# Fewer, larger tail loads in a pooling kernel, with one square moved to VectorE

## Chip, cores, metric

One core of a Trainium2 chip. Times are device microseconds of a whole execution; the profile's span is some 1.7 to 1.8 us shorter. Every run was fast, with a granted clock of 1.0.

## The reference

```python
x: (32, 256, 4096) float32, p = 2.0, kernel_size = 4
for i in range(out_length):
    window = np.abs(x[:, :, 4 * i:4 * i + 4]) ** p
    result[:, :, i] = (np.mean(window, axis=-1)) ** (1.0 / p)
```

Each output is the root of the mean of four squares. It reads 134.22 MB and writes 33.55 MB.

## The kernel before

The input is cut into 20 slots of at most 13184 columns on 128 partitions, which rotate through three SBUF tiles. ScalarE (ACT) squares in place, VectorE (DVE) sums fours, ACT takes the root of a whole group (`groups` says how many loads make one), and the result is stored. An odd piece (840 columns' worth, laid out as 3584 columns on 30 partitions) goes first.

```python
slots = [[(W, [W])]] * 17 + [[(W, [6592, 6592])]]            # W = 13184
slots += [[(6592, [6592]), (6592, [6592])], [(6592, [6592]), (4216, [2112, 2104])]]
ODD = 840
groups = [2] * 9 + [3, 1]
late = {7, 8, 9, 10}            # groups whose store waits on the load queue, after all loads
in_x = {9: (2, 0), 10: (2, 4944)}
FINE, ENDS, LAG = {21}, {19, 20}, 1
PAIRS = 15                      # from this load on: two pairwise adds instead of a reduce
# ...
for i in range(n):
    s, _, w, chunks = loads[i]
    while ahead < n and loads[ahead][0] < s + X_SLOTS:
        load(ahead)             # one DMA on the sync queue
        ahead += 1
    # ...
    for step in chunks:
        v = xs[i][:, c:c + step]
        r = nc.scalar.activation(out=v, in_=v, func=Act.Square)
        # ...
        total_sum(ots[g][:, summed:summed + step // k], v, i)
        while pending and pending[0][0] <= done - LAG:
            root(*pending.pop(0)[1:])
        # ...
for job in pending:
    root(*job[1:])
for g in sorted(late):
    store(g, nc.sync)
```

The tail, which the change touches, is the last two slots (numbers 18 and 19) and the four late stores.

Of the kernel before, what the change touches and what calls it, by code (L numbers as in the profile page):

```python
# [1 line left out]

# [4 lines left out]


@with_exitstack
def kernel(  # L10
    ctx: ExitStack,
    tc: tile.TileContext,
    x: bass.AP,
    p: float,
    kernel_size: int,
    out: bass.AP,
):








    nc = tc.nc

    assert float(p) == 2.0, "kernel specialized for p == 2"
    k = int(kernel_size)
    assert k == 4, "kernel specialized for kernel_size == 4"  # L30

    P = nc.NUM_PARTITIONS
    fp32 = mybir.dt.float32
    Act = mybir.ActivationFunctionType
    xf = x.rearrange("b c l -> (b c l)")
    of = out.rearrange("b c l -> (b c l)")
    total = xf.shape[0] // P

    W, O_W = 13184, 6592
    X_SLOTS, O_SLOTS = 3, 2  # L40
    slots = [[(W, [W])]] * 17 + [[(W, [6592, 6592])]]
    slots += [[(6592, [6592]), (6592, [6592])], [(6592, [6592]), (4216, [2112, 2104])]]
    ODD = 840
    groups = [2] * 9 + [3, 1]
    late = {7, 8, 9, 10}
    in_x = {9: (2, 0), 10: (2, 4944)}
    FINE, ENDS, LAG = {21}, {19, 20}, 1
    PAIRS = 15


    loads = [(s, sum(w for w, _ in slot[:j]), *slot[j]) for s, slot in enumerate(slots)
             for j in range(len(slot))]
    n = len(loads)
    assert sum(w for _, _, w, _ in loads) + ODD == total

    firsts = [sum(groups[:g]) for g in range(len(groups))]
    assert sum(groups) == n
    group_of = [g for g, count in enumerate(groups) for _ in range(count)]
    columns = [sum(w for _, _, w, _ in loads[firsts[g]:firsts[g] + groups[g]])
               for g in range(len(groups))]  # L60

    x_pool = ctx.enter_context(tc.tile_pool(name="x_pool", bufs=1))
    o_pool = ctx.enter_context(tc.tile_pool(name="o_pool", bufs=1))

    x_tiles = [x_pool.tile([P, W], fp32, name=f"xt{j}") for j in range(X_SLOTS)]
    o_tiles = [o_pool.tile([P, O_W], fp32, name=f"ot{j}") for j in range(O_SLOTS)]
    ctx.enter_context(tc.manual_schedule())

    def block(flat, g, div):
        at, width = sum(columns[:g]) * P // div, columns[g] * P // div  # L70
        return flat[at:at + width].rearrange("(p w) -> p w", p=P)

    xs = {}
    by_load = []

    def load(i):
        s, at, w, _ = loads[i]
        v = x_tiles[s % X_SLOTS][:, at:at + w]
        g = group_of[i]
        src = sum(loads[j][2] for j in range(firsts[g], i))  # L80
        nc.sync.dma_start(out=v, in_=block(xf, g, 1)[:, src:src + w])  # L81
        xs[i] = v

    ots = {}




    stores = {}
    by_act = []  # L90
    sums = []

    def follows(ins, before):
        for b in before:
            tc.declare_no_dep(ins.ins, b.ins, reason="follows from other waits")

    def store(g, queue):
        stores[g] = queue.dma_start(out=block(of, g, k), in_=ots[g])  # L98

    def root(g, o, ends):  # L100
        r = nc.scalar.activation(out=o, in_=o, func=Act.Sqrt, scale=1.0 / k)  # L101
        follows(r, by_act[:-1] + list(stores.values()))
        by_act.append(r)
        if ends and g not in late:
            store(g, nc.scalar)

    def total_sum(o, v, i):
        add = mybir.AluOpType.add
        if i < PAIRS:
            r = nc.vector.tensor_reduce(  # L110
                out=o, in_=v.rearrange("p (n j) -> p n j", j=k),
                axis=mybir.AxisListType.X, op=add,
            )
            follows(r, sums[:-1])
            sums.append(r)
            return

        q = v.rearrange("p (n j) -> p n j", j=k)
        front = v[:, 0:v.shape[1] // 2]
        h = front.rearrange("p (n j) -> p n j", j=2)  # L120
        r = nc.vector.tensor_tensor(out=h, in0=q[:, :, 0:2], in1=q[:, :, 2:4], op=add)  # L121
        follows(r, sums[:-1] + by_load)
        r = nc.vector.tensor_tensor(out=o, in0=h[:, :, 0], in1=h[:, :, 1], op=add)  # L123
        follows(r, sums[:-1])
        sums.append(r)


    Q = 30
    odd = ODD * P // Q
    t = o_tiles[1][0:Q, 0:odd]  # L130
    nc.sync.dma_start(out=t, in_=xf[(total - ODD) * P:total * P].rearrange("(p w) -> p w", p=Q))  # L131
    ahead = 0
    while ahead < n and loads[ahead][0] < X_SLOTS:
        load(ahead)
        ahead += 1
    nc.vector.tensor_tensor(out=t, in0=t, in1=t, op=mybir.AluOpType.mult)  # L136
    o = o_tiles[1][0:Q, odd:odd + odd // k]
    nc.vector.tensor_reduce(  # L138
        out=o, in_=t.rearrange("p (n j) -> p n j", j=k),
        axis=mybir.AxisListType.X, op=mybir.AluOpType.add,  # L140
    )
    nc.scalar.activation(out=o, in_=o, func=Act.Sqrt, scale=1.0 / k)  # L142
    stores["odd"] = nc.scalar.dma_start(
        out=of[(total - ODD) * P // k:total * P // k].rearrange("(p w) -> p w", p=Q), in_=o,
    )
    pending = []
    done = 0
# [3 lines that stand above are left out]
            load(ahead)  # L151
            ahead += 1
        g = group_of[i]
        if i == firsts[g]:
            t, first = (o_tiles[g % O_SLOTS], 0) if g not in in_x else (x_tiles[in_x[g][0]], in_x[g][1])
            ots[g] = t[:, first:first + columns[g] // k]
            summed = rooted = 0
        assert sum(chunks) == w
        c = 0
        for step in chunks:  # L160
            v = xs[i][:, c:c + step]
            r = nc.scalar.activation(out=v, in_=v, func=Act.Square)  # L162
            follows(r, by_act[:-1])
            by_act.append(r)
            total_sum(ots[g][:, summed:summed + step // k], v, i)
            while pending and pending[0][0] <= done - LAG:
                root(*pending.pop(0)[1:])
            done += 1
            c += step
            summed += step // k  # L170
            ends = summed == columns[g] // k
            if ends or i in FINE or (i in ENDS and c == w):
                pending.append((done - 1, g, ots[g][:, rooted:summed], ends))
                rooted = summed
# [6 lines that stand above are left out]
# [1 line left out]
_INS = ['x', 'p', 'kernel_size']  # L182
_OUTS = [((32, 256, 1024), 'float32')]

_NUMBERS = {'p': 2.0, 'kernel_size': 4}


# [26 lines left out]
```

## Time and profile before

| | before |
|---|---|
| time, median of the first 3 runs | 395.49 us (394.0 to 395.52) |
| profiled run, its span | 394.21 us, 392.4 us |
| DVE / ACT busy | 268.5 us (68%) / 280.2 us (71%) |
| bytes moved, mean rate | 167.77 MB, 428 GB/s |
| DMAs | 35 |

To read it: neither compute engine is full, the DMA engines are from start to end (share 1.00 at 432 GB/s from 2 to 388 us), and 167.77 MB at the rate the windows show fill the span. The lines stand in the prediction below.

### The profile page before, as it was taken

The numbers are of one execution on the slowest core, as the hardware profiler recorded it, in microseconds if no ns is written. First come the engines' busy times: TensorE is split into PE (matmuls) and PEld (weight loads), VectorE is DVE, ScalarE is ACT, GpSimd is POOL, SyncE is SP. The second block draws the span as 40 slices with busy tenths as digits, with TensorE's granted clock in tenths as the row PEclk, the third lists the DMA queues.
The fourth block names the chain that finished last, engine by engine and source line by source line (L and its number), as shares of the span: only waits on it lengthen the run. The fifth ranks groups of instructions, "written<-read, shape, count | busy, mean of one in ns | idle before, by whom it ended". The sixth has DMA issues, their size and how long they took to land.

```text
span 392.4 us, 183 instructions
## 1 busy us (share of the span) xinstructions
DVE 268.5 (68%) x35; ACT 280.2 (71%) x39; POOL 0.2 (0%) x4
## 2 busy tenths in 40 slices
DVE  4307898885769476948693769396928690989481
ACT  1085879919990899099909990998099919999991
POOL 0000000000000000000000000000000000000000
DMA  8999999999999998999999999999999999999997
GB/s 318 425 441 430 446 441 441 411 435 470 430 398 430 473 430 387 430 473 430 411 441 438 430 473 425 392 430 430 430 435 452 446 430 446 409 430 416 446 430 321
DMA packets 4842, 167.77 MB, mean 428 GB/s; under 512 B 558, under 2 KB 558, under 8 KB 716
## 3 DMA queue, kind: packets, MB, share of 16 engines
q1 hardware_dynamic: 3789, 144.04, 85.3%
q10 hardware_dynamic: 1053, 23.73, 14.0%
HBM read 134.22 MB, written 33.55 MB: 428 GB/s over the span
## 4 chain that ended last, share of the span: by engine, by line
DMA 47%; ACT 34%; DVE 16%; SPq 0%; ACTq 0%; issue 0%
DMA xt<-in_x_dram 47%; ACT xt L162 28%; DVE ot L110 14%; ACT ot L101 6%; DVE xt L121 1%; DVE xt L123 1%; ACT xt L101 1%; ACTq L98 0%; SPq L81 0%; SPq L131 0%
## 5 line engine op out<-in xcount | busy, mean ns | idle before, releaser
L162 ACT ACTIVATE xt<-xt 128x13184 f32<-128x13184 f32 (+3 forms) x24 | 222.2, 9272 | 91.4 <-DMA xt<-in_x_dram 89.8
L110 DVE TENSOR_REDUCE ot<-xt 128x3296 f32<-128x13184 f32 x15 | 208.3, 13886 | 88.6 <-ACT xt L162 88.6
L101 ACT ACTIVATE ot<-ot 128x6592 f32<-128x6592 f32 x9 | 51.1, 5681 | 0.0
L121 DVE TENSOR_TENSOR xt<-xt 128x3296 f32<-128x3296 f32 (+3 forms) x9 | 34.5, 3836 | 22.5 <-ACT xt L162 22.2
L123 DVE TENSOR_TENSOR ot<-xt 128x3296 f32<-128x3296 f32 (+1 forms) x4 | 10.9, 2734 | 0.1
L142 ACT ACTIVATE ot<-ot 30x896 f32<-30x896 f32 x1 | 0.9, 948 | 10.9 <-DVE ot L138 10.9
L101 ACT ACTIVATE xt<-xt 128x3296 f32<-128x3296 f32 (+3 forms) x4 | 5.8, 1449 | 2.3 <-DVE xt L123 2.3
L136 DVE TENSOR_TENSOR ot<-ot 30x3584 f32<-30x3584 f32 x1 | 3.9, 3879 | 5.1 <-DMA ot<-in_x_dram 5.1
L123 DVE TENSOR_TENSOR xt<-xt 128x1648 f32<-128x1648 f32 (+2 forms) x5 | 7.0, 1407 | 0.2
L138 DVE TENSOR_REDUCE ot<-ot 30x896 f32<-30x3584 f32 x1 | 3.9, 3874 | 0.0
L142 ACT ACT_TABLE_LOAD x1 | 1.3, 1283 | 0.7 <-PEq L195 0.7
L195 POOL MEMSET const-bfloat16-1.0<- 128x1 bf16 x1 | 0.1, 101 | 0.0
L195 POOL MEMSET const-uint8-127<- 128x1 uint8 x1 | 0.1, 101 | 0.0
L195 POOL MEMSET const-float32-0.0<- 128x1 f32 x1 | 0.1, 98 | 0.2 <-issue 0.2
L195 POOL MEMSET const-float32-1.0<- 128x1 f32 x1 | 0.1, 98 | 0.0
## 6 DMA issues: line engine op xcount, KB each, us to landing
xt<-in_x_dram SPq DMA_DIRECT2D x18, 6592.0 KB, 31.3
out_dram<-ot ACTq DMA_DIRECT2D x7, 3296.0 KB, 27.0
xt<-in_x_dram SPq DMA_DIRECT2D x3, 3296.0 KB, 24.2
out_dram<-ot SPq DMA_DIRECT2D x2, 3296.0 KB, 26.2
out_dram<-xt SPq DMA_DIRECT2D x1, 2472.0 KB, 9.2
xt<-in_x_dram SPq DMA_DIRECT2D x1, 2108.0 KB, 23.7
out_dram<-xt SPq DMA_DIRECT2D x1, 527.0 KB, 5.9
ot<-in_x_dram SPq DMA_DIRECT2D x1, 420.0 KB, 4.3
```

What stands on the lines that cost most here:

```text
L101: r = nc.scalar.activation(out=o, in_=o, func=Act.Sqrt, scale=1.0 / k)
L110: r = nc.vector.tensor_reduce(out=o, in_=v.rearrange("p (n j) -> p n j", j=k), axis=mybir.AxisListType.X, op=add,)
L121: r = nc.vector.tensor_tensor(out=h, in0=q[:, :, 0:2], in1=q[:, :, 2:4], op=add)
L123: r = nc.vector.tensor_tensor(out=o, in0=h[:, :, 0], in1=h[:, :, 1], op=add)
L136: nc.vector.tensor_tensor(out=t, in0=t, in1=t, op=mybir.AluOpType.mult)
L138: nc.vector.tensor_reduce(out=o, in_=t.rearrange("p (n j) -> p n j", j=k), axis=mybir.AxisListType.X, op=mybir.AluOpType.add,)
L142: nc.scalar.activation(out=o, in_=o, func=Act.Sqrt, scale=1.0 / k)
L162: r = nc.scalar.activation(out=v, in_=v, func=Act.Square)
L195: nc = _bacc.Bacc("TRN2", target_bir_lowering=False, num_devices=1)
```

## The change

The intent: half as many loads in the tail, with the time that ACT loses by waiting for a whole slot bought back on VectorE, which squares part of slot 18 while ACT squares the rest; the root of the group ahead is put behind that square. (`LAGS` says by how many squares the root of a group is put off: 2 for group 8, else 1. `FINE` and `ENDS` cut the last roots into smaller ones, and `in_x` gives the last outputs a place in an input tile that is done with.)

```diff
-    slots += [[(6592, [6592]), (6592, [6592])], [(6592, [6592]), (4216, [2112, 2104])]]
+    slots += [[(W, [5792, 7392])], [(10808, [6592, 2808, 1408])]]
-    groups = [2] * 9 + [3, 1]
+    groups = [2] * 9 + [1, 1]
-    in_x = {9: (2, 0), 10: (2, 4944)}
-    FINE, ENDS, LAG = {21}, {19, 20}, 1
+    in_x = {9: (2, 0), 10: (2, 3296)}
+    FINE, ENDS, LAGS = {19}, {18}, {8: 2}
+    ON_DVE = {(18, 0)}
 ...
-            r = nc.scalar.activation(out=v, in_=v, func=Act.Square)
-            follows(r, by_act[:-1])
-            by_act.append(r)
+            if (i, c) in ON_DVE:
+                r = nc.vector.tensor_tensor(out=v, in0=v, in1=v, op=mybir.AluOpType.mult)
+                follows(r, sums[:-1])
+            else:
+                r = nc.scalar.activation(out=v, in_=v, func=Act.Square)
+                follows(r, by_act[:-1])
+                by_act.append(r)
             total_sum(ots[g][:, summed:summed + step // k], v, i)
-            while pending and pending[0][0] <= done - LAG:
+            while pending and pending[0][0] <= done - LAGS.get(pending[0][1], 1):
```

## The prediction

> **What bounds the kernel now.** I read the page from the top: the engine shares, the row of slices, then the end of the span in the timeline and in windows. The two compute engines are far from full, and the DMA row is not:
>
> ```profile
> DVE 268.5 (68%) x35; ACT 280.2 (71%) x39; POOL 0.2 (0%) x4
> ...
> DMA  8999999999999998999999999999999999999997
> ...
> DMA packets 4842, 167.77 MB, mean 428 GB/s; under 512 B 558, under 2 KB 558, under 8 KB 716
> ...
> DMA 47%; ACT 34%; DVE 16%; SPq 0%; ACTq 0%; issue 0%
> ```
>
> The fourth line is the chain of waits. It credits ACT with a third of the span, which tempts one to shorten ACT. But the DMA engines are full in every slice except the first and last, during those ACT stretches too. So I cut the span into windows (columns: window, its length, DVE, ACT and POOL busy with counts, clock, DMA share, GB/s):
>
> ```profile
> 2.00:388.00 386.00, 268.45 (x35) 278.97 (x39) 0.00 (x0) 1.00 1.00 432
> ```
> ```profile
> 356.00:369.00 13.00, 7.12 (x4) 13.00 (x4) 0.00 (x0) 1.00 1.00 430
> 369.00:377.00 8.00, 7.88 (x3) 8.00 (x3) 0.00 (x0) 1.00 0.99 425
> 377.00:384.00 7.00, 5.35 (x5) 5.68 (x4) 0.00 (x0) 1.00 0.98 422
> 384.00:388.00 4.00, 0.93 (x2) 0.64 (x1) 0.00 (x0) 1.00 1.02 440
> ```
>
> From 2 to 388 us the DMA share is 1.00 at 432 GB/s, and the tail itself (356 to 388) has no gap. 167.77 MB / 432 GB/s = 388.4 us. Start-up is about 2 us (first load issued at 0.73), and what follows the last bytes about 2 us (202 GB/s from 390 to 391 us, nothing from 391 to the end at 392.4). 2 + 388.4 + 2 = 392.4, the whole span. The kernel is bound by bytes, from end to end; compute is hidden except for its last store's issue.
>
> The tail has a queue of stores waiting behind the loads, which is why it has no gap (columns: start, duration, instruction):
>
> ```profile
> 345.56 17.58 SPq L98 DMA_DIRECT2D out_dram<-ot  x2
> ...
> 373.92 2.95 ACT L101 ACTIVATE xt<-xt 128x3296 f32<-128x3296 f32 x1
> ...
> 381.11 4.88 SPq L98 DMA_DIRECT2D out_dram<-xt  x2
> ...
> 385.00 0.64 ACT L101 ACTIVATE xt<-xt 128x526 f32<-128x526 f32 x1 [1.53 <-DVE xt L123]
> ```
>
> The last four stores leave at 345.6, 362.8, 381.1 and 385.7 us. The last load (2108 KB, issued about 345.0) lands 23.7 us later, at 368.7. After it there are 3.375 + 3.375 + 2.53 + 0.54 MB of stores; at 432 GB/s, taken in the order of issue, they finish at 376.5, 384.3, 390.2 and 391.4. The measured landing of the last is 5.9 us after 385.66 = 391.6, so this simple queue reproduces the end of the kernel. Each store is in the queue before the one ahead of it has drained: by 31, 14, 3.2 and 4.5 us.
>
> [...] 432 GB/s sustained with loads and stores mixed, loads alone or stores alone. [...]
>
> **The change part by part.** The instruction order on every engine is identical up to the two squares of the 6592-column halves of the last full slot (ACT at 340.2, DVE adds ending 357.04). So every load is issued when it was: the slot it goes into is freed by the same sums (323.7 and 344.6 us). What changes is the tail.
>
> 1. *Loads.* Slot 18 comes as one 13184-column load instead of two halves, slot 19 as one of 10808 instead of 6592 + 4216. The bytes are the same. 35 DMAs become 33. In the old kernel the halves of slot 18 landed at 347.9 and 355.8 (28.0 us is the median of the pair; 24.2 is the first). Now all of it lands at 355.8, and all of slot 19 at 368.7 instead of its first half some 5 us sooner. Cost to ACT: after its second half-square ends at 351.5 it now waits to 355.8, 4.3 us.
>
> 2. *Square of 5792 columns moves to DVE.* [...] 6.19 us of new DVE time, against two ACT squares of 6592 (11.3 us) replaced by one of 7392 ([...] 6.34 us): ACT is given back 5.0 us, which about pays for the wait in 1.
>
> 3. *Root of the group ahead goes behind the 7392 square.* Its sums end at 357.04, in the middle of that square. ACT: square 355.8 to 362.2, root of 6592 (5.68) to 367.8, a short wait for slot 19, square of 6592 from 368.7 to 374.4. In the old kernel the same square ended at 373.95. Store of this group: 367.9 instead of 362.8, still 8 us before the store ahead of it has drained (376.5).
>
> 4. *DVE.* Square 357.07 to 363.26, adds of 2896 and 1448 (3.17 + 1.67) to 368.2, adds of 3696 and 1848 (4.01 + 2.08) to 374.3. This ends just as ACT finishes the 6592 square, so the root of 3296 columns follows with at most a few tenths of waiting: 374.4 to 377.3, and its store (1.69 MB) leaves at 377.4 instead of 381.1.
>
> 5. *Last load's end.* DVE adds for the 6592 chunk: 374.4 + 3.59 + 1.87 = 379.9. ACT squares 2808 from 377.2 to 379.8, roots 1648 from 379.9 to 381.5, squares 1408 to 382.8. DVE adds 1404 and 702 (1.62 + 0.89) by 382.5, then 704 and 352 (0.89 + 0.52) from 382.8 to 384.2. Roots of 702 and 352 end at 383.5 and 384.7. Last store issued about 384.75, against 385.66: 0.9 us sooner, but it is larger, 1.38 MB instead of 0.54.
>
> 6. *The queue.* Loads end at 368.7; stores drain at 376.5, 384.3, 388.2 (1.69 MB, 3.9 us) and 391.4 (1.38 MB, 3.2 us). The last store is in the queue 3.5 us before the one ahead has drained. A transfer needs about 1 us from issue to its first bytes (0.73 to the 1.6 to 1.8 us window at the start), so no gap opens. The end stays where the bytes put it.
>
> Sum: ACT +4.3 - 5.0, DVE +6.2 - about 1, last issue -0.9 us, all beside a full DMA; on the path that sets the end: 0. Two DMAs fewer may save a few hundredths.
>
> **The rivals.** (a) *Compute sets the end.* The chain of waits ends in ACT, and if the last issue really set the end, 0.9 us sooner would show as 391.5, a gain of 0.2%. Against it: 422 to 440 GB/s in the tail, and the last store's 5.9 us, where 0.54 MB need 1.25. (b) *The larger last store is late and the queue runs dry.* It has 3.5 us, less about 1 us to its first bytes, so 2.5 us to lose. A new wait is possible where ACT waits for DVE at 374.3; an upset of 1 us there stays hidden. Even an idle DMA at issue would give 384.75 + 1 + 3.2 + about 2 = 391, no later than now. A loss of 2% (7.9 us) would need the chain to slip by over 8 us. (c) *Whole-slot loads with rows of 52 KB move faster than 26 KB rows.* Against it: windows of half-slot loads (356 to 369) run at 430, the long stretch of whole-slot loads at 432. If true, 12 MB at 1% more is 0.3 us. (d) *The coarser loads starve ACT.* True for 4.3 us, but nothing downstream empties the queue; for it to matter the store at 367.9 must come after 376.5.
>
> **Range and chances.** The span should be 392.4 with half a microsecond either side. The four times of the kernel before (395.52, 395.49, 394.0, profiled 394.21) have a mean of 394.8 and spread 1.5 us. I take 394.8, and 393.3 to 396.6 for 8 times in 10: below, rivals (a) and (c) together on a good run; above, the high pair plus a gap of 1 us. Faster by 2% would need 387.6 us, below what 167.77 MB take at 432 GB/s plus start and end: 1%. Slower by 2%: 1.5%. Within 2%: 97.5%.
>
> **What would show each step right or wrong.** DMA share 1.00 and about 432 GB/s from 2 to 388 us again, no window in the tail under about 400. ACT idle some 4.3 us behind slot 18 (step 1); DVE's square of 5792 columns at 6.19 us (step 2); the two last stores issued near 377.4 and 384.75 (steps 4, 5), the very last landing some 6 to 7 us after its issue. A landing of only 4 to 5 us would mean the queue had run dry. I am wrong if the tail windows show a DMA gap, if slot 18 or 19 lands later than 355.8 and 368.7, or if the rate itself changes.

The new lengths in steps 2 to 5 can be had from the profile before alone, as estimates. VectorE's adds of 528, 1648 and 6592 columns take 707, 1874 and 7025 ns there; the line through the shortest and the longest (1.042 ns a column) gives 6.19 us for 5792 columns, if a product takes as long as an add. ScalarE's squares of 2112 and 6592 columns take 1947 and 5684 ns, and the line through them gives 6.35 us for 7392, where the prediction has 6.34. The few hundredths for two DMAs fewer are an estimate too: the trace before has 558 packets of 4 bytes, 9 ns each (median), for 35 DMAs, some 16 for each, so two DMAs fewer are two such packets less on each of 16 engines, 0.02 us.

## The result

| | before | changed |
|---|---|---|
| median (range), runs | 394.19 (394.0 to 395.52), 6 | 394.01 (393.62 to 395.11), 6 |
| ratio changed / before, 95% interval | | 0.9988 [0.9967, 1.0008] |

Ratios are the mean of one kernel's fast runs over the mean of the other's of the same rounds, so not quite the ratio of the medians. The changed kernel takes the same time. Both kernels' runs fall in two bands, near 394 and near 395.3; the profile of the changed kernel fell on a run of the upper one (395.11 us, span 393.3), which has to be kept in mind when it is set beside the profile before (394.21).

The page of the changed kernel, the lines that answer to those of before (engine shares, DMA row of the 40 slices, DMA sums, chain of waits by engine):

```profile
DVE 274.5 (70%) x36; ACT 275.4 (70%) x38; POOL 0.2 (0%) x4
...
DMA  8999999999989999999999999999999899999996
...
DMA packets 4554, 167.77 MB, mean 427 GB/s; under 512 B 526, under 2 KB 526, under 8 KB 556
...
DMA 54%; ACT 25%; DVE 19%; SPq 0%; issue 0%; ACTq 0%
```

VectorE gained 6.0 us and ACT lost 4.8 us. The chain of waits moved 9% of the span from ACT to other entries, and nothing came of it: the DMA row is as full as it was. The windows (length; DVE, ACT, POOL busy; clock; DMA share; GB/s):

```profile
2.00:388.00 386.00, 274.46 (x36) 274.09 (x38) 0.00 (x0) 1.00 1.00 432
356.00:369.00 13.00, 12.90 (x5) 11.95 (x2) 0.00 (x0) 1.00 1.01 437
369.00:377.00 8.00, 7.75 (x4) 7.23 (x2) 0.00 (x0) 1.00 0.98 422
377.00:384.00 7.00, 6.48 (x5) 6.71 (x5) 0.00 (x0) 1.00 0.99 426
384.00:388.00 4.00, 1.33 (x2) 1.06 (x2) 0.00 (x0) 1.00 1.00 425
```

432 GB/s from 2 to 388 us again, and no window of the tail below 422. The same bytes at the same rate take the same time. Four lines of the timeline of the changed tail (start, duration, instruction, idle time before it and what ended it):

```profile
356.99 6.36 ACT L167 ACTIVATE xt<-xt 128x7392 f32<-128x7392 f32 x1 [4.28 <-DMA xt<-in_x_dram]
358.16 6.18 DVE L164 TENSOR_TENSOR xt<-xt 128x5792 f32<-128x5792 f32 x1
...
378.33 7.92 SPq L99 DMA_DIRECT2D out_dram<-xt  x2
...
385.40 0.50 ACT L102 ACTIVATE xt<-xt 128x352 f32<-128x352 f32 x1 [0.84 <-DVE xt L124]
```

ACT waits 4.28 us for the whole of slot 18 (4.3 was predicted) and VectorE's new square takes 6.18 us (6.19). Everything sits about 1 us later than the plan, because this run's slot 18 landed about 1 us late (why, below); in the profiles of runs near 394 (below) the ACT square starts at 355.7 to 356.0 and the last store leaves at 384.6 and 384.9, for 384.75 predicted.

### The profile page after: what moved, and what is told of

It reads as the page before. It is cut to its first block, busy times and chain, and to the rows that moved or that the text cites. A ratio compares the mean times of both kernels' runs of the same rounds, so it can differ in the third digit from the quotient of the medians.

```text
span 393.3 us, 182 instructions
## 1 busy us (share of the span) xinstructions
DVE 274.5 (70%) x36; ACT 275.4 (70%) x38; POOL 0.2 (0%) x4
## 2 busy tenths in 40 slices
DMA packets 4554, 167.77 MB, mean 427 GB/s; under 512 B 526, under 2 KB 526, under 8 KB 556
## 4 chain that ended last, share of the span: by engine, by line
DMA 54%; ACT 25%; DVE 19%; SPq 0%; issue 0%; ACTq 0%
DMA xt<-in_x_dram 54%; ACT xt L167 22%; DVE ot L111 14%; DVE xt L122 3%; ACT ot L102 3%; DVE ot L124 1%; DVE xt L124 1%; ACT xt L102 1%; SPq L82 0%; ACTq L99 0%; SPq L132 0%
## 5 line engine op out<-in xcount | busy, mean ns | idle before, releaser
L167 ACT ACTIVATE xt<-xt 128x13184 f32<-128x13184 f32 (+4 forms) x23 | 217.4, 9458 | 97.9 <-DMA xt<-in_x_dram 96.2
L122 DVE TENSOR_TENSOR xt<-xt 128x3296 f32<-128x3296 f32 (+5 forms) x9 | 34.5, 3834 | 16.9 <-ACT xt L167 16.8
L124 DVE TENSOR_TENSOR xt<-xt 128x1448 f32<-128x1448 f32 (+4 forms) x5 | 7.0, 1409 | 0.2
L164 DVE TENSOR_TENSOR xt<-xt 128x5792 f32<-128x5792 f32 x1 | 6.2, 6184 | 0.0
```

The lines of the kernel that those rows point to most:

```text
L122: r = nc.vector.tensor_tensor(out=h, in0=q[:, :, 0:2], in1=q[:, :, 2:4], op=add)
L124: r = nc.vector.tensor_tensor(out=o, in0=h[:, :, 0], in1=h[:, :, 1], op=add)
L164: r = nc.vector.tensor_tensor(out=v, in0=v, in1=v, op=mybir.AluOpType.mult)
```

## The experiments

Theory: bytes set the end. The late stores keep the DMA engines supplied, so anything that compute does in the tail is free until the last store leaves too late to reach the queue before it has drained. Main rival: compute sets the end, as the chain of waits suggests. Twelve runs, in three sets; each set shares its runs of the kernel before. At a threshold of 2% every one of them counts as the same time as before. The intervals of four lie clear of 1 (8.0 us of idle work, whole tail loads alone, quarters, 13 KB pieces); of the others, medians and profiles are read together.

| run | median us (n) | before, same set | ratio to before, 95% |
|---|---|---|---|
| changed, again | 394.01 (6) | 394.49 (11) | 0.9988 [0.9964, 1.0011] |
| 2.0 us of idle ACT work | 394.11 (6) | 394.49 | 0.9987 [0.9966, 1.0007] |
| 8.0 us of idle ACT work | 399.33 (4) | 394.49 | 1.0114 [1.0090, 1.0139] |
| compute made thin | 394.24 (6) | 394.49 | 0.9984 [0.9966, 1.0002] |
| whole tail loads alone | 397.44 (6) | 394.41 (11) | 1.0066 [1.0047, 1.0084] |
| root ahead moved back | 395.05 (6) | 394.41 | 1.0008 [0.9987, 1.0029] |
| loads in quarters | 397.32 (5) | 394.41 | 1.0066 [1.0046, 1.0085] |
| 3.8 us of idle ACT work | 395.14 (6) | 394.41 | 1.0011 [0.9993, 1.0029] |
| 13 KB pieces, same DMAs | 397.17 (6) | 394.60 (11) | 1.0065 [1.0042, 1.0088] |
| no odd piece | 395.24 (6) | 394.60 | 1.0008 [0.9992, 1.0024] |
| root ahead moved back, again | 394.45 (6) | 394.60 | 0.9990 [0.9972, 1.0008] |
| changed, a third time | 393.97 (6) | 394.60 | 0.9986 [0.9969, 1.0004] |

### Compute made thin

Every square, sum and root is cut to 8 or 2 columns; all loads and stores stay. The results are wrong on purpose.

```diff
+    for ot in o_tiles:
+        nc.vector.memset(ot, 1.0)
-            v = xs[i][:, c:c + step]
+            v = xs[i][:, c + step - 8:c + step]
-            total_sum(ots[g][:, summed:summed + step // k], v, i)
+            total_sum(ots[g][:, summed + step // k - 2:summed + step // k], v, i)
     def root(g, o, ends):
+        o = o[:, o.shape[1] - 2:o.shape[1]]
```

> All loads and stores as in the changed kernel, but every square, sum and root works on 8 (2) columns only: wrong results on purpose, compute next to nothing. Theory (bytes set the time): 393.5 to 394.2 us, at most half a microsecond below the changed kernel. Rival (the compute chain sets the end or starves the queue): 388 us or less.

Measured: 394.24 us, the same as with all the work (and 0.04 us above the range that the theory gave). The window of the profile with next to no compute:

```profile
2.00:388.00 386.00, 23.94 (x38) 6.94 (x38) 0.00 (x0) 1.00 1.00 432
```

23.94 us of DVE and 6.94 us of ACT in place of about 274 each, and still 432 GB/s. This is the floor for this set of transfers, and the changed kernel sits on it; the kernel before, whose tail is cut into other transfers, lies within 0.3 us of it in the median of the same set (394.49). The rival falls, and so does every hope of a faster version by rearranging compute alone.

### How much the last store has to spare: idle work ahead of the last root

```diff
     for job in pending:
+        d = x_tiles[0][:, 0:N]      # a finished slot; N = 2180, 4340, 9380
+        r = nc.scalar.activation(out=d, in_=d, func=Act.Square)
+        follows(r, by_act[:-1])
+        by_act.append(r)
         root(*job[1:])
```

> The changed kernel with one idle square of 2180 columns (2.0 us) put in ScalarE just ahead of the last root; it touches a finished slot, so results stay right. Theory (bytes set the end, the last store has about 2.5 us to spare): last store issued at 388 instead of 386, time unchanged within 0.3 us. Rival (the compute chain sets the end): plus 2.0 us, 396.0.

> The idle square ahead of the last root at 4340 columns (3.8 us). The run with 2.0 us moved the last issue by about 1 us only, as it filled a wait; the run with 8.0 us moved it by 7 and cost 5. Here the last issue should move by 2.9 us, to 387.8. Theory with 2 us to spare: plus 0.9 us, 394.9. With the 2.5 us of the prediction: plus 0.4. Rival (compute chain sets the end): plus 2.9, 396.9.

> The same with a square of 9380 columns (8.0 us). Theory: 2.5 us are hidden, 5.5 us show: about 399.5 us, with a gap in the DMA share near 388 to 394. Rival (the compute chain sets the end): plus 8.0, 402.0.

Measured: 394.11, 395.14 and 399.33 us. The first run is weaker than it was meant to be: the inserted square started in the 0.84 us that ACT waits for VectorE there anyway, so the last store left at 385.70 instead of 384.90, only 0.8 us later, and that was hidden. The second left at 388.32, the third at 391.51. The last store of the repeat of the changed kernel and of the run with 8.0 us:

```profile
384.90 0.33 SPq L99 DMA_DIRECT2D out_dram<-xt  x1
```
```profile
391.51 0.33 SPq L99 DMA_DIRECT2D out_dram<-xt  x1
```

Windows of 8.0 us, then of 3.8 us:

```profile
386.00:387.00 1.00, 0.00 (x0) 1.00 (x1) 0.00 (x0) 1.00 0.99 422
387.00:388.00 1.00, 0.00 (x0) 1.00 (x1) 0.00 (x0) 1.00 0.01 0
...
392.00:392.20 0.20, 0.00 (x0) 0.00 (x0) 0.00 (x0) 1.00 0.00 0
392.20:393.00 0.80, 0.00 (x0) 0.00 (x0) 0.00 (x0) 1.00 1.01 432
```
```profile
387.00:388.00 1.00, 0.00 (x0) 1.00 (x2) 0.00 (x0) 1.00 0.10 40
388.00:389.00 1.00, 0.00 (x0) 0.29 (x1) 0.00 (x0) 1.00 0.03 13
389.00:390.00 1.00, 0.00 (x0) 0.00 (x0) 0.00 (x0) 1.00 0.99 422
```

The first of these two fences gives two numbers: the queue ahead of the last store is empty at 387.0 us, and a store issued at 391.51 moves no bytes before 392.2. Windows of 0.1 us put its first bytes between 392.3 and 392.4, some 0.8 us after its issue. So a last store issued by about 387.0 - 0.8 = 386.2 opens no gap; the changed kernel issues it at 384.90, with 1.3 us to spare. In both gaps the DMA engines stand still for want of a store, and the times rise: of the 6.6 us by which the third run's store was late, 5.3 show in the medians; of 3.4 in the second, 1.1. The first fits the 1.3 us; the second is smaller than its gap of about 1.9 us, and its runs (394.44 to 395.9) overlap with those of the changed kernel. The 16 completion marks of the last store (packets of 4 bytes and 9 ns in the traces, some 16 for each transfer and so one for each of the 16 DMA engines: 558 before for 35 DMAs, 526 after for 33) offer a reason, though no run isolates it: without a gap they lie 0.6 to 0.9 us apart in runs near 394, after these two gaps only 0.15, so part of the gap is paid with unevenness that is there in any case.

### The changed kernel again, twice

> The changed kernel once more, unaltered. Theory (the bytes set the end): median within 0.3 us of 394.0, ratio to before 0.998 to 1.000. Its first profile fell on a run of 395.1 us in which about one engine's worth of traffic (9 GB/s on average from 391 to 393.3 us) was still under way after the rest had ended. If such a laggard makes the slower runs, a profile of a run near 394.0 shows nothing after 391.5 us, and one of a run near 395.2 shows some 27 GB/s (a sixteenth of 432) up to about 392. If not, the two kinds of run look alike at the end.

> The changed kernel unaltered, third time, as the partner of the run before: 394.0 median, within 0.3, with one or two of six runs near 395.2.

Measured: 394.01 and 393.97, with 2 of 6 runs above 395 each time. All three ratios to before are 0.9986 to 0.9988, a gain of some 0.1%, and every interval reaches past 1. The end of the first profile of the changed kernel (a run of 395.11), then of the repeat (394.08):

```profile
390.00:391.00 1.00, 0.00 (x0) 0.00 (x0) 0.00 (x0) 1.00 0.24 97
391.00:392.00 1.00, 0.00 (x0) 0.00 (x0) 0.00 (x0) 1.00 0.05 22
```
```profile
390.00:391.00 1.00, 0.00 (x0) 0.00 (x0) 0.00 (x0) 1.00 0.16 65
391.00:392.00 1.00, 0.00 (x0) 0.00 (x0) 0.00 (x0) 1.00 0.00 0
```

In the slower run 22 GB/s, a DMA share of 0.05, go on through 391 to 392: about one engine of sixteen (1/16 is 0.06). The completion marks agree: the last comes 1.87 us after the first there, the other fifteen within 0.38; in the two profiles near 394 the whole spread is 0.62 and 0.90. One engine that makes the spread about 1.1 us wider is as much as the band is slower. The loads show it too, and in more profiles: the marks of slot 18's load lie 1.1 to 2.8 us apart in the four profiles of runs from 394.95 to 395.89 us (this one, 3.8 us of idle work, no odd piece, and the first with the root moved back), and 0.6 to 0.9 us in the six of runs from 393.61 to 394.39. Nor does the lag arise at the end: in this run the last mark of a load follows the fifteenth by at most 0.3 us up to the load that is squared at 301.84, and by 1.3 to 1.6 us from the one squared at 323.68 on, which is why slot 18 came about 1 us late. So lagging engines go with the upper band in every profile here; what makes them lag is not shown. Slower runs come in both kernels, so the comparison doesn't hang on it.

### The whole tail loads alone

```diff
-    FINE, ENDS, LAGS = {19}, {18}, {8: 2}
+    FINE, ENDS, LAGS = {19}, {18}, {}
-    ON_DVE = {(18, 0)}
+    ON_DVE = set()
```

> The two whole tail loads alone: the square of 5792 columns goes back to ScalarE and the root of the group ahead waits behind one square again. Theory (bytes set the end, the last store has some 2 us to spare): ScalarE carries 5.0 us more after slot 18 lands at 355.9, the last store is issued near 389.4 instead of 384.9, 4.5 us later; 2 of these are hidden, so about 396.6 us, with a DMA gap near 388 to 390. Rival (compute is off the path altogether, whatever its order): 394.0. Rival (the compute chain sets the end): 398.5.

Measured: 397.44 us; the profiled run 396.23, the others 397.25 to 397.84. The profiled run's last store left at 389.02 (389.4 expected), and its windows show the gap:

```profile
387.00:388.00 1.00, 0.95 (x2) 0.66 (x1) 0.00 (x0) 1.00 0.04 13
388.00:389.00 1.00, 0.47 (x1) 0.50 (x1) 0.00 (x0) 1.00 0.00 0
389.00:390.00 1.00, 0.00 (x0) 0.00 (x0) 0.00 (x0) 1.00 0.38 162
```

So the merged loads by themselves cost about 3.4 us against the changed kernel, and the square on VectorE with its new order buys them back. The direction is the theory's; the size was 0.8 us short (396.6 expected). The shorter time to spare accounts for little of that: 4.1 us of delay less 1.3 would give 396.8. Why five runs took a further 1 to 1.6 us over the profiled one, which lies below even that, isn't settled.

### The root of the group ahead moved back

```diff
-    FINE, ENDS, LAGS = {19}, {18}, {8: 2}
+    FINE, ENDS, LAGS = {19}, {18}, {}
```

> Root of the group ahead back ahead of the 7392-column square; loads and the square on VectorE as in the changed kernel. Theory: ScalarE fills its wait with the root from 357.0, squares 7392 to 369, so VectorE's adds end near 375.1 and everything after is 0.7 us later, last store near 385.6; inside the 2 us to spare: time unchanged within 0.3 us of 394.0. Rival (compute chain sets the end): 394.7.

> The run with the root of the group ahead moved back, repeated beside the changed kernel in the same rounds. It took 395.05 where 394.0 was expected, with 5 of 6 runs in the upper of the two bands (395 and 394) that all versions show. If chance: median within 0.3 us of the changed kernel's. If moving the root costs: its last store is issued 0.7 us later and the queue runs dry for up to 0.5 us in slower runs, median 0.5 to 1.0 us above the changed kernel's in the same rounds.

Measured: 395.05, then 394.45 (the changed kernel in the second set: 393.97). The two profiles differ. In the first (394.95 us) slot 18 landed at 356.81, by its last completion mark, VectorE's square began at 357.98, the last store left at 386.54, and there is a small dip. In the second (393.61 us) the slot landed at 355.43, 1.4 us sooner, the store left at 385.14 and there is no dip:

```profile
387.00:387.50 0.50, 0.00 (x0) 0.00 (x0) 0.00 (x0) 1.00 0.82 343
```
```profile
387.00:387.50 0.50, 0.00 (x0) 0.00 (x0) 0.00 (x0) 1.00 1.08 454
```

In the second profile the last store leaves 0.5 us later than in the changed kernel of the same set (384.60), close to the 0.7 expected, and within the 1.3 us to spare. A run whose loads land late has less than that to spare and can run dry. Whether the order of the root is worth anything in the mean stays open: 395.05 missed the expectation by 1.0, 394.45 lies half a microsecond above the partner, and the intervals overlap.

### Loads in quarters, and small pieces without more DMAs

The medians of before and changed differ by 0.2 to 0.6 us in the three comparisons. Could that come from two DMAs fewer? First, each of the 19 whole-slot loads as four DMAs; then as one DMA whose source lies in four places, so that the pieces are as small and the DMAs as few as ever. Its output is wrong, which doesn't matter for the time.

```diff
-        nc.sync.dma_start(out=v, in_=block(xf, g, 1)[:, src:src + w])
+        parts = 4 if w == W else 1                                  # quarters
+        for k4 in range(parts):
+            a, b = w * k4 // parts, w * (k4 + 1) // parts
+            nc.sync.dma_start(out=v[:, a:b], in_=block(xf, g, 1)[:, src + a:src + b])
```
```diff
+        if w == W:                                                  # 13 KB pieces
+            at0 = (sum(columns[:g]) + src) * P
+            nc.sync.dma_start(out=v.rearrange("p (m w) -> p m w", m=4),
+                              in_=xf[at0:at0 + w * P].rearrange("(m p w) -> p m w", m=4, p=P))
```

> Each of the 19 loads of 13184 columns issued as four quarters (13 KB rows instead of 52 KB): 57 DMAs more, same bytes, compute unaltered. Theory (bytes at some 432 GB/s set the time; a DMA costs each engine one 4-byte packet of about 10 ns): at most plus 0.6 us, about 394.5. Rival (the few tenths between the two kernels come from two DMAs fewer, 0.1 to 0.2 us each): plus 6 to 11 us, 400 or more.

> The changed kernel with as many DMAs as it has (33), but each of the 19 loads of 13184 columns reads its 52 KB per partition from four places, in pieces of 13 KB; outputs land in other places, so results are wrong on purpose. The quarters run cost 3.3 us with 57 DMAs more and the same small pieces. If the cost is per DMA (0.058 us each): 394.0 here, within 0.4. If it is per piece: 397.3.

Measured: 397.32 and 397.17 us. The first missed both expectations: 3.3 us over the changed kernel, where 0.6 or at least 6 was expected. (The 4-byte packets of that expectation are in the traces, 9 ns each in the profile of the changed kernel; under 512 B there are 526 packets there and 1438 in quarters, so 57 more on each engine, which is 0.5 us.) The second tells the cause: with not one DMA more it costs the same. The packet lines of the changed kernel's repeat and of the 13 KB run, and the long window of the latter, with full DMA engines at a lower rate (430 for 432 GB/s):

```profile
DMA packets 4555, 167.77 MB, mean 428 GB/s; under 512 B 527, under 2 KB 527, under 8 KB 557
```
```profile
DMA packets 11850, 167.77 MB, mean 425 GB/s; under 512 B 526, under 2 KB 526, under 8 KB 556
```
```profile
2.00:388.00 386.00, 274.46 (x36) 274.06 (x38) 0.00 (x0) 1.00 1.01 430
```

7295 pieces more, 456 on each of 16 engines, for 3.2 us: 7 ns a piece. The packets themselves agree: in the traces one of 52 KB takes 1947 ns and one of 13 KB 493 ns (medians), so four small ones take 25 ns longer than a large one, 8 ns for each further piece. From the 7 ns, an estimate for the change itself: it removed 288 packets (4842 to 4554), 18 an engine, 0.13 us. That agrees in sign with what the medians show and is too small to be measured here.

### No odd piece

A try at a better version: the odd piece and its store folded into the last load, 31 DMAs.

```diff
-    slots += [[(W, [5792, 7392])], [(10808, [6592, 2808, 1408])]]
-    ODD = 840
+    slots += [[(W, [5792, 7392])], [(11648, [6592, 3304, 1752])]]
+    ODD = 0
-    (the load, square, sum, root and store of the odd piece)
```

> A try at a better one: the separate first piece of 840 columns on 30 partitions and its store are folded into the last load (11648 columns), 31 DMAs. Theory: two DMAs less save 0.12 us, the last store is issued about 0.6 us later, inside the time to spare: 393.8 us, not to be told from 394.0. Rival (the last issue has less to spare than that): 394.5 or more.

Measured: 395.24 us; the number is the one that the rival in the expectation gave. The 0.12 us for two DMAs fewer was an estimate from the quarters (3.3 us for 57 DMAs) and is not shown: the 13 KB run cost 3.2 us with no DMA more. The last store left at 387.02, not 385.5: in the profiled run (395.89 us) the last load itself came later (ACT's square of it starts at 370.23), and the queue ran dry sooner. That profile has the lag as well, with the last mark of this load 1.6 us after the fifteenth, so how much of the 1.3 us over the changed kernel of the same set (393.97) is due to the change isn't settled:

```profile
386.00:387.00 1.00, 0.39 (x1) 0.57 (x1) 0.00 (x0) 1.00 0.56 237
387.00:388.00 1.00, 0.00 (x0) 0.00 (x0) 0.00 (x0) 1.00 0.47 203
```

No version tried here beats the changed kernel, and the thin run says that none with these transfers will do so by more than noise.

## Why the prediction was right

- *Bytes set the end* (its first part and step 6): shown. The thin run takes 394.24 us without the compute, the profile after has 432 GB/s where the one before had it, and the median of 394.01 lies 0.8 us under the 394.8 predicted, inside the range. That 0.8 us comes mostly from how the centre was chosen: a mean of four runs, of which two were in the upper band.
- *Unchanged issue of the loads and ACT's wait* (step 1): shown, 4.28 us for 4.3.
- *The moved square* (step 2): 6.18 us for 6.19. The whole-loads-alone run shows that it is needed: without it and the new order, about 3.4 us are lost.
- *The root behind the square* (step 3): it causes no loss, as predicted, but that this order is better than the other is not shown.
- *VectorE and the end of the tail* (steps 4 and 5): last store at 384.90 and 384.60 in runs near 394, for 384.75.
- *The time to spare* (step 6 and rival b): mis-sized. The prediction put the end of the queue ahead of the last store at 388.2 us and its first bytes 1 us after issue, which gave 2.5 us. Measured: 387.0 and 0.8, which gives 1.3. It counted a landing as the end of the bytes, but the landing comes later: in the run with 8.0 us of idle work the store ahead has moved its bytes by 387.0 and lands at 387.9. So every drain time was about a microsecond late. The answer didn't need this term. For the experiments with 1.6 us of delay and more it mattered, but it is no sharp line: with 1.3 us the run of 8.0 us is met (399.3 for 399.33 us), while the one of 3.8 us should have taken 396.1 and took 395.14, and the whole loads alone 396.8 and took 397.44.
- *Its own signs of being wrong*: one of them fired. It called itself wrong if slots 18 and 19 landed later than 355.8 and 368.7; in the first profile of the changed kernel they landed at 356.96 and 369.75, by their last completion marks, in a run of the upper band (395.11 us), and the median still met the forecast. The sign left no room for the upper band; in the two profiles near 394 they landed at 355.93 and 368.73, and at 355.63 and 368.45. The other signs held: no tail window below 422 GB/s (400 was the limit), and the last landing 6.6 us after its issue (6 to 7).
- *Loose readings that changed nothing*: the DMA row before has an 8 in the 16th slice too, so the engines are not at 9 in all slices but the first and last. Stores alone run at 422 to 440 GB/s in the prediction's own windows, not at 432. And of "31, 14, 3.2 and 4.5 us" the first is the time to that store's own landing; the load ahead of it lands 23 us after its issue.
- *Rival (a)* fell with the thin run. *Rival (b)* was absent from the changed kernel's profile and appeared when the last store left after about 386.2 (a small dip at 386.54, none at 385.92). *Rival (c)*, larger pieces move faster, was argued against in the prediction, with 0.3 us at stake. It is true but tiny: 0.8% from 52 KB to 13 KB pieces, and 0.13 us for this change.
- *What the change does spend*, which the prediction didn't say: before, the last store left at 385.66 with the bytes of the store ahead ending near 389.3 (0.54 MB at 432 GB/s, 1.25 us, before the last bytes at about 390.5), so it had 389.3 - 0.8 - 385.66 = 2.8 us to spare, an estimate. The change left about half of that.

## What to carry to other kernels

When the DMA share is 1.00 at a steady rate from start to end (here at 432 GB/s from 2 to 388 us), cutting the compute to nothing while keeping the transfers is the one experiment that tells how much any rearrangement can bring; do it first. A chain of waits that names a compute engine doesn't contradict it: here it followed who waited, not what was scarce, and its 34% for ACT was worth nothing. In the tail of such a kernel ask how long before the queue drains the last store is issued, measure that by delaying it, and count from the last bytes, not from the landing (387.0 and 387.9 us for the store ahead in the run with 8.0 us of idle work).
